# Expert rows gathered from x in plain float32, the first token half ahead, in a two-layer decoder trunk

## The chip, the core and the metric

One core of one Trainium2 chip. The metric is device time in microseconds of one execution, the median over runs. The program has five engines' instruction streams: PE (matmuls; PEld is its weight load), DVE (VectorE), ACT (ScalarE), POOL (GpSimd) and SP (sync), which issues the weight transfers in order.

## What is computed

Two layers over 256 tokens of width 1024, all in float32: a GLA and sparse-attention layer with a dense SwiGLU, then a Mamba-2 layer with a mixture of experts, then a closing norm. The change touches the last block alone:

```python
shift, scale, gate = adaln(c, moe_mod_w[i], moe_mod_b[i])
ffn = moe_ffn(modulate(x, moe_norm[i], shift, scale), moe_router[i], moe_w_gu[i], moe_w_down[i])
x = x + (gate * ffn).astype(x.dtype)
...
return rmsnorm(x, final_norm)
```

`modulate` is `rmsnorm(x, w) * (1 + scale) + shift`, one factor per token (the norm) and one scale and shift per channel. `moe_ffn` sends each token to the two experts with the largest router logits, each a SwiGLU of 1024 to 2 x 3584 to 1024, weighted by a softmax over the two.

## The kernel before

A tile layer schedules each engine's stream by priority and dependence; the order shown below is what it made, and each engine runs its stream in order.

**Tokens and slots.** The 256 tokens lie as two halves b = 0, 1 of 128 partitions in `x`. For each half the router's logits L are ranked on DVE (`rk`), `mk` marks the two chosen experts and a small PE product with a triangular matrix (L1205, L1207) gives `po_`, a token's slot number within its expert. Experts are worked in eight places; place 0 is always expert 0, the others are sorted by load. A place has three or two groups of 32 slots in turn (`NGS`), so 96 or 64 columns.

**Gather.** `gather(places)` makes `sl`, a 0/1 matrix tokens x slots, from `po_` and `mk` (L1229), and multiplies it with the normed tokens: for each of 8 channel blocks k, `xnh` and `xnl` (x times the norm factor, split into a high and a low float32r part by ACT L1359 and DVE L1360) for both halves, four matmuls (L1237, L1238). ACT and DVE apply scale and shift and write `gx` (L1242, L1244). Then it turns `sl` into slot rows `stT` (L1256) and gathers the mixing weights `gs` (L1265), which only the scatter at an expert's end needs. Place 0 is gathered ahead of everything; places 1 and 2 during place 0, 3 and 4 during place 2, and so on.

**Experts.** For each place and each of four chunks of the hidden width, `gate_up` multiplies `gx` with the weights in blocks of 1 MiB (L1276, output pa), four 32-row strips side by side; then silu and product (`sg`), a transpose (`turn_a`, `at`, L1310), and `down` (L1276, output pb). A three-group place has 12 matmuls per block, a two-group place 8. Plain float32 matmuls show as two records each. Each place has 42 blocks, 336 in all.

**Weights.** `load` (L238) takes the next buffer of a ring and issues a transfer on SP, which waits in order for the buffer's last reader. The ring has 6 + 3 buffers through the program, and 5 more (`raw3`) when the last stage's space becomes free; so 14 in the expert stage.

**Start of the stage.** `logits` transposes x by PE (L1176), copies it to SBUF (L1177) and multiplies with the router (L1180), for two column halves of each token half, during the last projection (L267 to L269); `dgs` holds each half's norm factor.

Of the kernel before, what the change touches and what calls it, by code (L numbers as in the profile page):

```python
# [8 lines left out]
F32 = mybir.dt.float32  # L9
# [12 lines left out]
NE = 8  # L22

CHUNKS = (1024, 1024, 1024, 512)
NS = 32
# [160 lines left out]
def trunk_kernel(ctx: ExitStack, tc: tile.TileContext, d: dict, out: bass.AP):  # L186
# [1000 lines left out]
    raws.append((ctx.enter_context(tc.tile_pool(name="raw3", bufs=5, side="right")), 5))  # L1187
    with ExitStack() as mx:
# [3 lines left out]
        L, rk, mk, po_ = (late.tile([128, 2, 8], F32, name=n) for n in ("L", "rk", "mk", "po_"))  # L1192
        c1, c2 = (late.tile([128, 8, 8], F32, name=n) for n in ("c1", "c2"))
        pp = pbank("pa")
        for b in range(2):
# [8 lines left out]
            mk_last = V.tensor_scalar(mk[:, b], rk[:, b], 1.5, None, op0=OP.is_lt)  # L1204
# [9 lines left out]
        iota = K("iota")  # L1214
# [3 lines left out]
        at_place = {}  # L1218

        def gather(places):  # L1220

            m_, p_, g_ = (mk, po_, ge) if places == (0,) else (mkp, pop, gep)
            sl = mw.tile([128, 2, 5 * NS], F32R, name="sl", bufs=1)
            off = [sum(NGS[q] for q in places[:i]) * NS for i in range(len(places) + 1)]
            W = off[-1]
            for b in range(2):
                for i, e in enumerate(places):
                    n = NGS[e] * NS
                    at_place["sl"] = V.tensor_scalar(sl[:, b, off[i]:off[i] + n], iota[:, :n], p_[:, b, e:e + 1],  # L1229
                                                     m_[:, b, e:e + 1], op0=OP.is_equal, op1=OP.mult)  # L1230
# [14 lines left out]
            yield  # L1245

# [3 lines left out]
            col = lambda b, g: sl[:, b, g * NS:(g + 1) * NS].bitcast(F32)  # L1250
# [134 lines left out]
        for _ in first:  # L1385
            pass
# [49 lines left out]
        for e in range(NE):  # L1436
            nxt = iter(())
            if e % 2 == 0:
                nxt = gather(tuple(range(e + 1, min(e + 3, NE))))
# [160 lines left out]
```

## Time and profile before

| | us |
|---|---|
| median of 3 runs | 1467.97 |
| lowest and highest | 1464.98, 1468.71 |
| profiled execution, its own time | 1465.52 |
| its span on the core | 1463.7 |
| PE busy in the span | 1412.7 |
| DMA moved | 493.66 MB, mean 337 GB/s |

A timeline row reads: start, length in us, engine, line, operation, output<-input, shapes, count of records, and in brackets the idle time of the engine before it and what ended it. PE rows include the drain of the last matmul, so neighbours overlap. A busy PE is not PE at its peak.

### The profile page before, as it was taken

The page shows a single profiled execution, that of the slowest core. Times are in us where ns is not written, and L with a number is a line of the kernel's source. Part 1 is how long each engine was busy: PE and PEld are TensorE (multiplying, and loading weights), DVE is VectorE, ACT ScalarE, POOL GpSimd, SP SyncE. Part 2 cuts the span into 40 slices and gives each one's busy share as a digit, 9 for nine tenths or more (in the row PEclk, how much of TensorE's full clock was granted, in tenths as well). Part 3 has the DMA queues.
Part 4 walks back from the last instruction along what each step waited for, and adds up shares of the span by engine and source line. Part 5 has one row for each costly group of instructions (what it writes and reads, how often), then busy time and mean ns, then how long its engine had stood idle before and what let it go on. Part 6 is the DMA issues. An engine that isn't in the chain of part 4 may idle for free.

```text
span 1463.7 us, 28534 instructions
## 1 busy us (share of the span) xinstructions
PE 1412.7 (97%) x12241; PEld 802.4 (55%) x12241; DVE 561.8 (38%) x1090; ACT 437.0 (30%) x856; POOL 5.3 (0%) x13
## 2 busy tenths in 40 slices
PE   7999999999999999999999999999999998999995
PEld 6876799999799987633433334333334323343321
DVE  7897688885678777510010110010100100100102
ACT  5577554444667785211000001000001000010001
POOL 0000000000000000000000000000000000000000
PEclk9999999999999999899999999999999999999998
DMA  9886778976544434699999999999999999999993
GB/s 383 345 303 259 300 295 334 363 289 228 207 173 148 141 116 172 235 358 357 370 421 419 419 419 420 418 420 419 420 419 418 420 419 419 419 420 418 419 420 148
DMA packets 68964, 493.66 MB, mean 337 GB/s; under 512 B 7648, under 2 KB 7904, under 8 KB 9568
## 3 DMA queue, kind: packets, MB, share of 16 engines
q1 hardware_dynamic: 68832, 491.77, 83.9%
q8 instruction: 98, 1.61, 0.4%
q14 instruction: 34, 0.28, 0.0%
HBM read 490.70 MB, written 1.05 MB: 336 GB/s over the span
## 4 chain that ended last, share of the span: by engine, by line
PE 80%; DMA 14%; ACT 3%; DVE 2%; issue 1%; SPq 0%; DVEq 0%; ACTq 0%
PE pa L1276 27%; PE pb L1276 12%; DMA raw<-in_e_gu_dram 7%; PE pa L267 7%; PE pa L268 7%; PE pa L269 7%; DMA raw<-in_e_gl_dram 4%; PE pb L268 3%; PE pb L269 3%; PE pb L267 3%; DMA raw<-in_e_dn_dram 3%; PE pc L1348 2%; PE pc L1310 1%; PE pb L400 1%; ACT wh L252 1%
## 5 line engine op out<-in xcount | busy, mean ns | idle before, releaser
L1276 PE MATMUL pa<-raw,gx 128*32 128x512 f32 (+1 forms) x5120 | 510.2, 540 | 7.3 <-DMA raw<-in_e_gl_dram 5.1
L1276 PEld LDWEIGHTS pa<-raw,gx 128*32 128x32 f32 x5120 | 167.1, 110 | 310.7 <-issue 258.4
L1276 PE MATMUL pb<-raw,at 128*32 128x512 f32 x2240 | 252.9, 594 | 4.3 <-DMA raw<-in_e_dn_dram 4.2
L1458 DVE TENSOR_TENSOR sg<-sg,pa 128x256 f32<-128x256 f32 (+1 forms) x80 | 31.0, 388 | 481.0 <-ACT sg L1457 479.3
L253 DVE TENSOR_TENSOR wl<-raw,wh 128x1024 fp32r<-128x1024 f32 (+1 forms) x155 | 185.3, 1204 | 57.1 <-ACT wh L252 56.9
L252 ACT CAST wh<-raw 128x1024 fp32r<-128x1024 f32 (+1 forms) x155 | 159.1, 1036 | 122.6 <-PE pb L268 53.0
L1276 PEld LDWEIGHTS pb<-raw,at 128*32 128x32 f32 x2240 | 70.8, 110 | 160.7 <-issue 141.1
L1457 ACT ACTIVATE sg<-pa 128x256 f32<-128x256 f32 (+1 forms) x80 | 28.6, 358 | 432.3 <-PE pa L1276 432.3
L267 PE MATMUL pa<-hh,wh 128*128 128x256 f32 (+1 forms) x392 | 112.4, 289 | 1.9 <-ACT wh L252 1.0
L268 PE MATMUL pa<-hl,wh 128*128 128x256 f32 (+1 forms) x392 | 111.4, 285 | 0.8 <-DVE hl L386 0.8
L269 PE MATMUL pa<-hh,wl 128*128 128x256 f32 (+1 forms) x392 | 111.3, 285 | 0.0
L267 PE MATMUL pb<-hh,wh 128*128 128x256 f32 (+1 forms) x360 | 101.7, 283 | 1.9 <-ACT hh L380 1.9
L268 PE MATMUL pb<-hl,wh 128*128 128x256 f32 (+1 forms) x360 | 102.5, 285 | 0.1
L269 PE MATMUL pb<-hh,wl 128*128 128x256 f32 (+1 forms) x360 | 101.8, 283 | 0.0
L281 DVE SCALAR_TENSOR_TENSOR junk<-raw,scb 128x1024 bf16<-128x1024 f32 x72 | 87.7, 1218 | 1.4 <-DMA raw<-in_hyb_mod_dram 0.8
L267 PEld LDWEIGHTS pa<-hh,wh 128*128 128x128 f32 (+1 forms) x392 | 73.7, 189 | 5.6 <-ACT wh L252 2.5
L268 PEld LDWEIGHTS pa<-hl,wh 128*128 128x128 f32 (+1 forms) x392 | 74.2, 189 | 2.1 <-DVE hl L386 0.9
L269 PEld LDWEIGHTS pa<-hh,wl 128*128 128x128 f32 (+1 forms) x392 | 74.0, 189 | 0.8 <-DVE gu L629 0.3
L1311 ACT COPY at<-pc 128x512 f32<-128x512 f32 (+2 forms) x32 | 17.5, 546 | 184.5 <-PE pc L1310 184.5
L267 PEld LDWEIGHTS pb<-hh,wh 128*128 128x128 f32 (+1 forms) x360 | 68.3, 190 | 2.9 <-ACT hh L380 2.1
L268 PEld LDWEIGHTS pb<-hl,wh 128*128 128x128 f32 (+1 forms) x360 | 68.3, 190 | 2.0 <-DVE hl L386 1.5
L269 PEld LDWEIGHTS pb<-hh,wl 128*128 128x128 f32 (+1 forms) x360 | 68.3, 190 | 0.1
(424 smaller groups left out, 1486.4 us busy)
## 6 DMA issues: line engine op xcount, KB each, us to landing
raw<-in_e_gu_dram SPq DMA_DIRECT2D x192, 1024.0 KB, 19.7
raw<-in_e_dn_dram SPq DMA_DIRECT2D x112, 1024.0 KB, 19.8
raw<-in_e_gl_dram SPq DMA_DIRECT2D x32, 1024.0 KB, 19.9
raw<-in_d_gu_dram SPq DMA_DIRECT2D x22, 1024.0 KB, 7.2
raw<-in_s_in_dram SPq DMA_DIRECT2D x20, 1024.0 KB, 4.8
raw<-in_hyb_mod_dram SPq DMA_DIRECT2D x12, 1024.0 KB, 9.9
raw<-in_ssm_mod_dram SPq DMA_DIRECT2D x12, 1024.0 KB, 6.4
raw<-in_d_dn_dram SPq DMA_DIRECT2D x11, 1024.0 KB, 7.9
```

The lines of the kernel that those rows point to most:

```text
L252: hi_last[0] = S.copy(hi[:, :n], r)
L253: lo_last[0] = V.tensor_sub(lo[:, :n], r, hi[:, :n].bitcast(F32))
L267: PE.matmul(ps, a[0], b[0], start=start, stop=False, **kw)
L268: PE.matmul(ps, a[0], b[1], start=False, stop=False, **kw)
L269: return PE.matmul(ps, a[1], b[0], start=False, stop=stop, **kw)
L281: V.scalar_tensor_tensor(jk, r[:, q * D:(q + 1) * D], 1.0, scb, op0=OP.mult, op1=OP.mult, accum_out=macc[m][:, 2 * j + q:2 * j + q + 1])
L400: PE.matmul(ps[:, o_ + b * 128:o_ + (b + 1) * 128], x[:, b, k * 128:(k + 1) * 128], dg[b], start=True, stop=True)
L1276: up_last[0] = PE.matmul(ps[32 * j:32 * j + 32, :rhs.shape[1]], lhs, rhs, start=start, stop=stop)
L1311: (V.tensor_copy if i else S.copy)(at[:, i:i + n].rearrange("p a n -> p (a n)"), pt_[:, :n * 128])
L1348: PE.matmul(pso[b], at_place[e, q][:, h, b], p[:, q], start=i == 0, stop=i == 2 * n - 1)
L1457: last = act(sg[:, r, :w], pg[r][:, :w], AF.Silu)
L1458: V.tensor_mul(sg[:, r, :w], sg[:, r, :w], pg[r][:, w:2 * w])
```

## The change

- The ring's last pool gets 7 buffers, 16 in all. Space for it comes from `xnh` and `xnl`, which go, and from `sg` and `at`, which are single now.
- Place 0 no longer goes through `gather`. For each half, as soon as its slots are known, DVE makes `s0`, the slot matrix times the token's norm factor (L1216), and PE multiplies x itself with it in plain float32 (L1218, 8 matmuls a half into two banks that stay open over both halves). ACT and DVE write `gx` from the two banks (L1232, L1234).
- Place 0's slot rows and mixing weights (`back`) come after its first chunk (L1446 is the gate's product ahead of them, L1283 the slot rows, L1292 the weights).
- A copy of x, `xc`, is made on ACT (L1476), since experts add to x while later places are gathered. Later gathers use `xc` and `sr`, the slot matrix times the norm factor, in plain float32: two matmuls per channel block (L1261) in place of four. Places 1 and 2 are gathered from the second chunk on.
- A fallback branch for overfull experts follows suit; it is not taken here.

```diff
-    raws.append((ctx.enter_context(tc.tile_pool(name="raw3", bufs=5, side="right")), 5))
+    raws.append((ctx.enter_context(tc.tile_pool(name="raw3", bufs=7, side="right")), 7))
...
+        pg0 = [pbank("pb") for _ in range(2)]
+        s0 = mp.tile([128, 2, CAP], F32, name="s0")
+        rx = mp.tile([128, 2], F32, name="rx")
         pp = pbank("pa")
         for b in range(2):
...
+
+            V.tensor_scalar(mr[:, b], rk[:, b], 1.5, dgs[b][0], op0=OP.is_lt, op1=OP.mult)
             V.tensor_copy(po_[:, b], pp[:, 8 * b:8 * b + 8])
+            V.tensor_scalar(s0[:, b], iota[:, :CAP], po_[:, b, 0:1], mr[:, b, 0:1], op0=OP.is_equal, op1=OP.mult)
+            for k in range(KD):
+                PE.matmul(pg0[k // 5][:, k % 5 * CAP:(k % 5 + 1) * CAP], x[:, b, k * 128:(k + 1) * 128], s0[:, b],
+                          start=b == 0 and k % 5 == 0, stop=b == 1, skip_group_check=True)
...
+        for k in range(KD):
+            src = pg0[k // 5][:, k % 5 * CAP:(k % 5 + 1) * CAP]
+            if k % 2:
+                act(gx[:, 0, k], src, AF.Identity, bias=B[:, k:k + 1], scale=A[:, k:k + 1])
+            else:
+                V.tensor_scalar(gx[:, 0, k], src, A[:, k:k + 1], B[:, k:k + 1], op0=OP.mult, op1=OP.add)
+
+        xc = mp.tile([128, 2, D], F32, name="xc")
...
+            sl, off = slots(places)
+            W = off[-1]
+            sr = mw.tile([128, 2, 5 * NS], F32, name="sr", bufs=1)
+            for b in range(2):
+                V.tensor_scalar(sr[:, b, :W], sl[:, b, :W], rx[:, b:b + 1], None, op0=OP.mult)
             for k in range(KD):
                 if k % 2 == 0:
                     yield
-                pgx = pbank("pb" if places == (0,) and k % 4 > 1 else "pc")
-                ks = slice(k * 128, (k + 1) * 128)
+                pgx = pbank("pc")
                 for b in range(2):
-                    PE.matmul(pgx[:, :W], xnh[:, b, ks], sl[:, b, :W], start=b == 0, stop=False)
-                    PE.matmul(pgx[:, :W], xnl[:, b, ks], sl[:, b, :W], start=False, stop=b == 1)
+                    PE.matmul(pgx[:, :W], xc[:, b, k * 128:(k + 1) * 128], sr[:, b, :W], start=b == 0, stop=b == 1)
...
             yield
+            back(places, sl, off)
+
+        def back(places, sl, off):
...
-            at = mw.tile([128, 2 * NG, 128], F32, name="at")
+            at = mw.tile([128, 2 * NG, 128], F32, name="at", bufs=1)
...
-        first = gather((0,))
-        next(first)
-        xnh = mp.tile([128, 2, D], F32R, name="xnh")
-        xnl = mp.tile([128, 2, D], F32R, name="xnl")
-        for b in range(2):
-            for hf in range(2):
-                s = slice(hf * 512, hf * 512 + 512)
-                with tc.issue_after(ex_last[0].ins), tc.issue_after((at_place["sl"] if b or hf else mk_last).ins):
-                    act(xnh[:, b, s], x[:, b, s], AF.Copy, scale=dgs[b][0])
-                    V.scalar_tensor_tensor(xnl[:, b, s], x[:, b, s], dgs[b][0], xnh[:, b, s].bitcast(F32),
-                                           op0=OP.mult, op1=OP.subtract)
...
-                    if i == 2:
+                    if i == 2 and (e, c) != (0, 0):
                         next(nxt, None)
-                sg = mw.tile([128, NG, 256], F32, name="sg")
+                sg = mw.tile([128, NG, 256], F32, name="sg", bufs=1)
...
                 if (e, c) == (0, 0):
                     with tc.issue_after(up_last[0].ins):
                         moe_gate()
-                next(nxt, None)
+                        for b in range(2):
+                            S.copy(xc[:, b], x[:, b])
+                        back((0,), *slots((0,)))
+                else:
+                    next(nxt, None)
```

How the streams change, in the words of the two programs. PE at the router's last steps; `pb<-cs,x` is a transpose of x, `pc<-ra,hh` the router's product. Before:

```order
L1176 MATMUL pb<-cs,x 128x128 x4
L1205 MATMUL pa<-mk,cs 128x8
L1207 MATMUL pa<-mk,cs 128x8
L1365 MATMUL pa<-mk,cs 128x8
L1180 MATMUL pc<-ra,hh 128x8 x4
L1176 MATMUL pb<-cs,x 128x128 x4
L1180 MATMUL pc<-ra,hh 128x8 x4
L1237 MATMUL pc<-sl,xnh 128x96 x2
```

The same place after:

```order
L1176 MATMUL pb<-cs,x 128x128 x4
L1210 MATMUL pa<-mk,cs 128x8
L1212 MATMUL pa<-mk,cs 128x8
L1380 MATMUL pa<-mk,cs 128x8
L1176 MATMUL pb<-cs,x 128x128
L1180 MATMUL pc<-ra,hh 128x8 x4
L1176 MATMUL pb<-cs,x 128x128 x3
L1218 MATMUL pb<-s_6353,x 128x96 x5
L1180 MATMUL pc<-ra,hh 128x8 x4
```

One transpose of the last column half moved ahead of a router product, and five of the first token half's eight gather matmuls stand ahead of the other. PE from the end of the first gather to the end of expert 0's first chunk, before (`pa<-raw,gx` are the expert's blocks):

```order
L1238 MATMUL pb<-sl,xnl 128x96
L1256 MATMUL pc<-cs,sl 32x128 x16
L1276 MATMUL pa<-raw,gx 32x512
L1265 MATMUL pc<-ge,sl 32x1 x16
L1276 MATMUL pa<-raw,gx 32x512 x95
L1431 MATMUL pc<-cs,mac_moe 32x128 x16
L1237 MATMUL pc<-sl,xnh 128x160
```

And after:

```order
L1218 MATMUL pb<-s_6353,x 128x96 x3
L1210 MATMUL pa<-mk,cs 128x8
L1380 MATMUL pa<-mk,cs 128x8
L1218 MATMUL pb<-s_6353,x 128x96 x8
L1303 MATMUL pa<-raw,gx 32x512 x96
L1446 MATMUL pc<-cs,mac_moe 32x128 x16
L1283 MATMUL pc<-cs,sl 32x128 x8
L1303 MATMUL pa<-raw,gx 32x512
L1283 MATMUL pc<-cs,sl 32x128 x8
L1292 MATMUL pc<-ge,sl 32x1 x16
```

The slot rows moved behind the first 96 block matmuls, the gate's product with them. SP at the first loads into the new pool, with what each waits for, before:

```order
L238 DMA raw<-in_e_gu_dram 128x2048 [waits DMAHW3_49,PE_49,Pool_49]
L238 DMA raw<-in_e_gu_dram 128x2048 [waits DMAHW4_49]
L238 DMA raw<-in_e_gu_dram 128x2048 [waits DMAHW5_49]
L238 DMA raw<-in_e_gu_dram 128x2048 [waits DMAHW6_49]
L238 DMA raw<-in_e_gu_dram 128x2048 [waits DMAHW7_49]
L238 DMA raw<-in_e_gu_dram 128x2048 [waits DMAHW0_49,PE_49]
L238 DMA raw<-in_e_gu_dram 128x2048 [waits DMAHW1_49,PE_49]
L238 DMA raw<-in_e_dn_dram 128x2048 [waits DMAHW2_49,PE_49]
```

And after:

```order
L238 DMA raw<-in_e_gu_dram 128x2048 [waits DMAHW3_49,PE_49,Pool_49]
L238 DMA raw<-in_e_gu_dram 128x2048 [waits DMAHW4_49]
L238 DMA raw<-in_e_gu_dram 128x2048 [waits DMAHW5_49]
L238 DMA raw<-in_e_gu_dram 128x2048 [waits DMAHW6_49]
L238 DMA raw<-in_e_gu_dram 128x2048 [waits DMAHW7_49]
L238 DMA raw<-in_e_gu_dram 128x2048 [waits DMAHW0_49]
L238 DMA raw<-in_e_gu_dram 128x2048 [waits DMAHW1_49]
L238 DMA raw<-in_e_dn_dram 128x2048 [waits DMAHW2_49,PE_49]
```

The sixth and seventh load into the pool lost their wait for PE; the eighth keeps one, on a buffer of an earlier pool.

## Rows read from the trace of the kernel before

**Rows 1.** Table of stretches: us, busy per engine, granted clock, DMA share, GB/s

```profile
605.00:610.00 5.00, 5.00 (x74) 3.21 (x77) 2.95 (x17) 3.39 (x6) 0.00 (x0) 0.52 0.10 39
610.00:615.00 5.00, 5.00 (x52) 1.80 (x48) 2.83 (x16) 0.00 (x0) 0.00 (x0) 1.00 0.30 87
...
610.00:730.00 120.00, 119.91 (x1287) 45.80 (x1283) 12.76 (x46) 12.51 (x31) 0.00 (x0) 1.00 0.92 352
730.00:1443.00 713.00, 695.81 (x6771) 243.23 (x6763) 73.42 (x160) 60.74 (x142) 0.00 (x0) 1.00 1.01 416
```

**Rows 2.** The chain that ended last, its end: start, us, what

```profile
1423.51 20.45 DMA raw<-in_e_dn_dram
...
1444.00 1.97 PE pb L1276 x16
```

**Rows 3.** Waits of the sync queue, 580 to 615: us in total, times, longest

```profile
SPq L238 <- PE pa L269: 11.2, 1, 11.2
...
SPq L238 <- PE pa L1276: 20.4, 2, 18.3
```

**Rows 4.** Timeline of the sync queue, expert 0 and the turn to expert 1

```profile
612.40 2.90 SPq L238 DMA_DIRECT2D raw<-in_e_gu_dram  x2
617.55 8.05 SPq L238 DMA_DIRECT2D raw<-in_e_dn_dram  x4
...
733.62 5.48 SPq L238 DMA_DIRECT2D raw<-in_e_dn_dram  x4
```

**Rows 5.** Line L238, the loads, from 520 to 640: issue to landing

```profile
DMA to landing us min/median/max: 4.7/5.0/13.3
```

**Rows 6.** Timeline of PE in expert 0: a gather step, four blocks, slot rows

```profile
643.93 0.34 PE L1237 MATMUL pc<-sl,xnh 128*128 128x160 f32 x1
...
644.78 0.28 PE L1238 MATMUL pc<-sl,xnl 128*128 128x160 f32 x1
644.98 10.51 PE L1276 MATMUL pa<-raw,gx 128*32 128x512 f32 x96
...
689.53 1.06 PE L1256 MATMUL pc<-cs,sl 128*32 128x128 f32 x32
...
691.84 0.58 PE L1265 MATMUL pc<-gep,sl 128*32 128x1 f32 x48
```

**Rows 7.** Timeline of PE at the router's last steps and the first block

```profile
592.54 1.06 PE L1180 MATMUL pc<-ra,hh 128*128 128x8 f32 x8
...
594.87 1.06 PE L1180 MATMUL pc<-ra,hh 128*128 128x8 f32 x8 [0.78 <-DVE hh L1177]
...
607.29 1.06 PE L1276 MATMUL pa<-raw,gx 128*32 128x512 f32 x1
```

**Rows 8.** Timeline of DVE, the second half's rank chain

```profile
592.33 0.68 DVE L454 TENSOR_TENSOR x<-x,res 128x512 f32<-128x512 f32 x1
594.12 0.69 DVE L1177 COPY hh<-pb 128x512 f32<-128x512 f32 x1 [1.11 <-PE pb L1176]
...
595.97 0.23 DVE L1196 TENSOR_REDUCE L<-pc 128x8 f32<-128x64 f32 x1 [1.08 <-PE pc L1180]
...
598.02 0.17 DVE L1204 TENSOR_SCALAR mk<-rk 128x8 f32<-128x8 f32 x1
...
599.12 0.32 DVE L1229 TENSOR_SCALAR sl<-cs,po__6347,mk 128x96 fp32r<-128x96 f32 x1
```

**Rows 9.** Timeline of PE, plain float32 matmuls L400 at two places

```profile
8.49 6.43 PE L400 MATMUL pb<-dg,x 128*128 128x128 f32 x32 [8.49 <-DVE dg L390]
...
182.33 1.16 PE L400 MATMUL pb<-dg,x 128*128 128x128 f32 x8
```

**Rows 10.** Table of stretches around the fall and rise of the clock

```profile
596.00:597.00 1.00, 0.43 (x2) 0.46 (x3) 0.93 (x5) 0.73 (x2) 0.00 (x0) 0.59 1.07 451
...
609.00:610.00 1.00, 1.00 (x31) 0.60 (x33) 0.33 (x4) 0.73 (x1) 0.00 (x0) 0.58 0.00 0
```

**Rows 11.** Costliest groups: ACT's cast of 128x1024

```profile
L252 ACT CAST wh<-raw 128x1024 fp32r<-128x1024 f32 (+1 forms) x155 | 159.1, 1036 | 122.6 <-PE pb L268 53.0
```

More of the change, by code (lines that the diff above doesn't have):

```diff
@@ L1190, in trunk_kernel @@
         mw = mx.enter_context(tc.tile_pool(name="moew", bufs=2))
-        L, rk, mk, po_ = (late.tile([128, 2, 8], F32, name=n) for n in ("L", "rk", "mk", "po_"))
+        L, rk, mk, mr, po_ = (late.tile([128, 2, 8], F32, name=n) for n in ("L", "rk", "mk", "mr", "po_"))
         c1, c2 = (late.tile([128, 8, 8], F32, name=n) for n in ("c1", "c2"))
+        iota = K("iota")
+        pg0 = [pbank("pb") for _ in range(2)]
+        s0 = mp.tile([128, 2, CAP], F32, name="s0")
+        rx = mp.tile([128, 2], F32, name="rx")
         pp = pbank("pa")
@@ L1218, in trunk_kernel, with slots, gather @@
         at_place = {}
[L1220 to L1223 removed]
+        for k in range(KD):
[5 more added lines that the diff above has]
+        xc = mp.tile([128, 2, D], F32, name="xc")
+        def slots(places):
+            m_, p_ = (mk, po_) if places == (0,) else (mkp, pop)
+            sl = mw.tile([128, 2, 5 * NS], F32, name="sl", bufs=1)
             off = [sum(NGS[q] for q in places[:i]) * NS for i in range(len(places) + 1)]
[L1225 removed]
             for b in range(2):
                 for i, e in enumerate(places):
[L1228 to L1230 removed]
+                    V.tensor_scalar(sl[:, b, off[i]:off[i + 1]], iota[:, :off[i + 1] - off[i]], p_[:, b, e:e + 1],
+                                    m_[:, b, e:e + 1], op0=OP.is_equal, op1=OP.mult)
+            return sl, off
+        def gather(places):
+            sl, off = slots(places)
[3 more added lines that the diff above has]
+                V.tensor_scalar(sr[:, b, :W], sl[:, b, :W], rx[:, b:b + 1], None, op0=OP.mult)
             for k in range(KD):
@@ L1383, in trunk_kernel @@
             V.scalar_tensor_tensor(ge[:, b], f0[:, b], v0[:, 0, b:b + 1], tm[:, b], op0=OP.mult, op1=OP.add)
-        for _ in first:
-            pass
+        for b in range(2):
+            V.tensor_copy(rx[:, b:b + 1], dgs[b][0])
         nt = mp.tile([128, 8], F32, name="nt")
@@ L1436, in trunk_kernel @@
         for e in range(NE):
-            nxt = iter(())
-            if e % 2 == 0:
-                nxt = gather(tuple(range(e + 1, min(e + 3, NE))))
+            nxt = gather(tuple(range(e + 1, min(e + 3, NE)))) if e % 2 == 0 else iter(())
             if e:
@@ L1461, in trunk_kernel @@
                         moe_gate()
-                next(nxt, None)
+                        for b in range(2):
+                            S.copy(xc[:, b], x[:, b])
+                        back((0,), *slots((0,)))
+                else:
+                    next(nxt, None)
                 if prev:
@@ L1489, in final @@
             y = [x_rstd(0)]
[L1490 removed]
+            jk = mw.tile([128, 512], F32, name="sg", bufs=1)
             V.scalar_tensor_tensor(jk, x[:, 1, h1], 1.0 / D, x[:, 1, h1], op0=OP.mult, op1=OP.mult,
@@ L1527, in trunk_kernel @@
                         for b in range(2):
-                            PE.matmul(pgx[:, :128], xnh[:, b, ks].bitcast(F32), s2[:, b], start=b == 0, stop=False)
-                            PE.matmul(pgx[:, :128], xnl[:, b, ks].bitcast(F32), s2[:, b], start=False, stop=b == 1)
+                            PE.matmul(pgx[:, :128], xc[:, b, ks], s2r[:, b], start=b == 0, stop=b == 1)
                         V.tensor_scalar(g2[:, k], pgx[:, :128], A[:, k:k + 1], B[:, k:k + 1], op0=OP.mult, op1=OP.add)
```

17 lines of the change are left out of this document (9 added, 8 removed).

## The prediction

> **What bounds the kernel now.** I read the table of stretches first. From 730 to 1443 us the DMA share is 1.01 and 416 GB/s are moved; from 610 to 730 it is 0.92 and 352, and in 605 to 615 the share is 0.10 and 0.30 [rows 1]. The chain of waits ends in the same sense: its last long pieces are transfers of 20 us, and after the last one only 16 matmul records and the closing norm remain [rows 2]. So from 730 us on, the end is a fixed distance behind the weight stream: 336 transfers of 1 MiB, 2.52 us each at 416 GB/s. Nothing that PE, ACT or DVE save there counts. What counts is how much transfer time is lost before the stream runs without holes. That loss lies in 596 to 735 us. The DMA queue's own waits show it: the sync queue stood 11.2 us until the last projection matmul L269, which frees the space of the new buffers, issued five loads, and then stood 20.4 us in two waits for the first expert's matmuls L1276 [rows 3]: all 14 buffers were full and none free.
>
> Behind that hole PE is the pace. The timeline of the sync queue has issues at 612.40 and, two to a 2.90 us row of which the last 0.33 is the issue itself, every 2.57 us; four dn loads take 8.05 us, the same 2.57 [rows 4]. That is one 1 MiB block of a three-group expert on PE: 96 records of L1276 (four blocks of 12 matmuls, two records each) take 10.51 us with the drain of the last [rows 6]. It is slower than the 2.52 us of a transfer, and gathers and transposes come on top, so in all of expert 0 each load is issued when PE frees a buffer, and lands 4.7 to 5.0 us later [rows 5]. At 733.62 the spacing has become 1.72 us [rows 4], the two-group expert 1, and the transfers are again the slower ones. A load n is therefore issued when block n minus the number of buffers is done, and the end of the kernel moves with that.
>
> **Part by part.**
>
> *Two more weight buffers (14 to 16).* Load n waits for block n-16, no longer for block n-14, and those are two blocks of 2.57 us apart on PE: 5.1 us earlier for every load of the PE-paced stretch. The order of the sync queue shows that both are usable at once: the two extra loads carry no wait for PE, and the load ahead of the seven waits for the same instruction as before. They fill the 10 us hole, in which 5.0 us of transfer fit. The space paid for them costs nothing on the path: sg and at, now single, are each written only when PE's own order has their last reader behind it. **+5.1 us.** Bounds: 0 (a rival below) and 5.1.
>
> *First expert's rows earlier.* Before, b=1's router logits (second L1180 at 594.87) lead over DVE's rank chain (595.97, 598.02) to the slot matrix at 599.12 [rows 7, 8]; then 32 matmuls over the two halves hi and lo, then the transposed slot rows L1256 and L1265, and the first L1276 at 607.29 [rows 7]. In the new order one transpose stands ahead of the first L1180 of b=1 and has to wait for x, ready at 593.01 (592.33 + 0.68), where L1180 began at 592.54; this shifts the hh copy of 594.12 by some 0.5 us [rows 7, 8]. Five of the new first-half matmuls then stand ahead of the second L1180. A plain float32 matmul of this form costs 0.25 us at full clock: L400, 8 records for 4 matmuls in 1.16 us, less the last record's drain; at the program's start 32 records (16 matmuls) took 6.43 us, 0.40 each [rows 9]. So the second L1180 goes from 594.87 to about 595.9, and b=1's slot matrix, which has one more small DVE operation ahead of it in the chain and the mr one, from 599.12 to about 600.4, done at 600.7. Eight matmuls remain: 2.0 us at full clock, 3.3 at low, and expert 0 starts at 602.7 or 604.1. DVE's first gx piece stands behind some ten small operations of 0.15 to 0.2 us and is ready at about 602.5, so it is not later than PE; the other seven are needed one per block.
>
> The clock decides what that start is worth. The granted clock fell at 596.2 (0.59 over 596 to 597), after PE had gaps between the router's steps, and was back at 609.8 (0.58 over 609 to 610) [rows 10]: 13.7 us at 1.2 instead of 2.4 GHz, through narrow matmuls, and up again 2.5 us after the first expert matmul. The second free buffer came at 614.97; two blocks of 2.57 back is 609.8, the start that before is worth at full clock. For the changed kernel I take the same rise, 2.5 us after the start at 604.1: half of 2.5 us is lost, so it is worth a start at 605.4. **+4.4 us.** Bounds: 7.1 (no fall: 602.7) and 1.1 (the clock falls in the new gap at about 599.6 and stays low for the same 13.7 us, to 613.3: 604.1 + 4.6 = 608.7).
>
> *First slot rows deferred.* They do not vanish: 16 L1256 and 16 L1265 now stand in PE's stream after expert 0's first chunk, where PE is the pace. The later set of 24 and 24 gives the price: 32 records of L1256 in 1.06 us, and two thirds of 0.58 [rows 6]. **-1.5 us**; up to -2.5 if PE also stands for the two pc banks that ACT empties between them. The two xc copies (ACT, 128x1024) stand between the router's copies, where ACT waits for PE and DVE, and cost nothing; were that cover gone, one pass of 1.04 us (a cast of that size [rows 11]) would go onto the start.
>
> *Gathers of experts 1 and 2.* Each of four steps runs 8 single-pass matmuls from 643.93 to 644.98, 1.05 us [rows 6]. Now 4 plain float32 ones; scaled by columns from L400, 0.25 x 160/128 = 0.31 us each, 1.25 us. Four steps lose 0.2 to 0.25 each: **-1.0 us.** Bounds: 0 (same time as now) and -3.8 (0.40 us as at low clock, 0.50 scaled, 2.0 a step). The Trainium skill, page "FP8 and Floating Point Precision", section "TensorE Precision Notes", says that true FP32 takes 4 passes through the array, which speaks against this change: two such matmuls would be eight passes where four single ones stood. By that rule alone a step doubles and the four lose 4.2 us, sum 3.8; the trace does not bear it out at this width, since L400's plain float32 matmul, of 128 columns, takes 0.25 us against 0.13 for one of the four single ones. The later gathers (experts 3 to 7) lie under the transfers: free.
>
> *Removed work on ACT and DVE* (xnh, xnl: four passes each): it was on the path to the first gather and is inside the start term; elsewhere it is hidden.
>
> **Sum:** 5.1 + 4.4 - 1.5 - 1.0 = 7.0 us. Against the profiled execution: span 1463.7 to 1456.7, time 1465.5 to 1458.5. That execution lies 2.5 us under the median of the three runs; from the median 1468.0 the forecast is **1461.0 us**. The next thing late is then still PE's pace in expert 0, up to about 730 us.
>
> **Rivals.**
> 1. *The clock does not fall, or returns within the gather:* the new first-half matmuls close PE's gap at 594 to 596, where it fell. For: dense float32 work stands there. Against: a new idle of about 2.5 us before b=1's matmuls. Start 7.1: gain 9.7, **1458.3**.
> 2. *The low clock only moves:* it falls in that new idle and lies on the expert's own blocks for as long as before. Start 1.1: gain 3.7, **1464.3**.
> 3. *PE sets the end, not the transfers:* PE reads 119.91 of 120 us and 695.81 of 713 us busy [rows 1]; then buffers bring nothing and only 4.4 - 2.5 is left, **1466.1**. Against it: a DMA share of 1.01 and the transfers in the chain.
> 4. *Plain float32 at twice the time:* PE holds the buffers of expert 0 for 3.2 us more, gain 3.8, **1464.2**. Against: the L400 row.
> 5. *Slower:* the low clock holds on through expert 0's first chunk. A block at half clock costs 5.15 instead of 2.57 us and each microsecond of it loses half. With 2.5 us against for the moved work and 5.1 for the buffers, the gain is gone if it lasts 16.6 us from 604.1, to 620.7; over the whole chunk of eight blocks it loses 20.6 and gives about **1480**. For: nothing but the fall itself; against: before, it rose 2.5 us after these same matmuls began.
>
> That the buffers or the early half are not really early is shut out by the order of the two programs.
>
> **How the numbers follow.** Forecast 0.50, rival 1 0.15, rival 2 0.17, rival 3 0.08, rival 4 0.05, rival 5 0.05. The forecast's own range is 1458.5 to 1463.5. For 8 in 10 the range takes in rivals 1 and 2 and the scatter of the runs before (1465.0 to 1468.7), and most of rival 3: 1456 to 1466. 0.3% is 4.4 us, about what a measurement of this kernel tells from no change: under 1463.6 is faster. Faster: the forecast, rival 1, and the better edge of 2: 0.70. Same: most of 2, 3 and 4: 0.25. Slower: 0.05.
>
> **What the profile will show.** The sync queue's wait for L1276 in 600 to 615 falls from 20.4 to under 10 us, with seven loads, not five, issued behind L269. First expert matmul at 602.5 to 604.5, after 16 new float32 matmuls. The clock row says which rival holds: low till about 606.6 for the forecast. The gather steps of expert 0 at 1.2 to 1.3 us, the moved slot rows after the eighth block. DMA share 1.01 reached some 7 us earlier in the program and unchanged after. Wrong would be: holes in the stream after 740 us, a first expert matmul later than 606, or an end that does not follow the last transfer by the same 20 us.

## The result, and the profile after

| | before | after |
|---|---|---|
| median of 18 runs each, side by side | 1468.84 | 1461.37 |
| lowest and highest | 1463.66, 1472.81 | 1456.38, 1467.96 |
| ratio, 95% interval | | 0.995 (0.9936 to 0.9964) |
| profiled execution: its time, its span | 1465.52, 1463.7 | 1462.21, 1460.3 |
| the same once more (e11, e12): time, span | 1465.01, 1463.0 | 1454.99, 1453.1 |

The forecast was 1461.0 with a range of 1456 to 1466. The whole interval of the ratio lies below 0.997, so by the bound of 0.3% the change is faster. In a later session the changed kernel had 1459.1 against 1469.84, ratio 0.9932 (0.9909 to 0.9954).

The stretches of the changed kernel (columns as in [rows 1]):

```profile
605.00:610.00 5.00, 4.50 (x24) 4.24 (x28) 2.77 (x20) 0.20 (x1) 0.00 (x0) 0.50 1.00 424
610.00:615.00 5.00, 5.00 (x36) 1.30 (x40) 4.13 (x21) 2.79 (x5) 0.00 (x0) 0.74 0.92 387
610.00:730.00 120.00, 120.00 (x1314) 44.77 (x1314) 17.52 (x68) 16.33 (x39) 0.00 (x0) 0.99 0.93 358
730.00:1443.00 713.00, 702.46 (x6821) 248.25 (x6818) 74.17 (x164) 61.44 (x143) 0.00 (x0) 1.00 1.00 415
```

Against [rows 1], the hole is gone: in 605 to 615 the DMA share is 1.00 and 0.92 where it was 0.10 and 0.30. The new buffers came free 4.3 us later in this execution than in that of before (more on this below), so the 30 us from there on, before and after, tell it better:

```profile
591.50:621.50 30.00, 27.76 (x244) 17.80 (x246) 15.94 (x74) 9.16 (x19) 0.00 (x0) 0.77 0.71 278
```

```profile
595.80:625.80 30.00, 27.95 (x202) 15.87 (x204) 13.22 (x69) 6.57 (x13) 0.00 (x0) 0.77 0.97 385
```

The share rose from 0.71 to 0.97. The long stretch is as before, 415 GB/s. The sync queue's waits in 590 to 618, to be read beside [rows 3], and its timeline, beside [rows 4]:

```profile
SPq L238 <- PE pa L1303: 16.9, 2, 14.8
SPq L238 <- PE pa L269: 11.2, 1, 11.2
```

```profile
595.80 3.41 SPq L238 DMA_DIRECT2D raw<-in_e_gu_dram  x7
614.07 8.05 SPq L238 DMA_DIRECT2D raw<-in_e_dn_dram  x4
624.37 22.21 SPq L238 DMA_DIRECT2D raw<-in_e_gu_dram  x8
```

Seven loads go out at 595.80, not five, and the first load that needs a freed buffer goes out at 614.07. The expert's matmuls, L1276 before, are L1303 now.

One thing must be known before spans are compared. Executions of one and the same program differ by several us ahead of all that the change touches: the release of the new buffers, the first issue behind L269, came at 591.50 and 591.61 in the two of before, at 595.80 and 591.54 in the two of after. In the first of after the clock is at half in four short stretches far upstream, three of them here:

```profile
87.00:91.00 4.00, 4.00 (x35) 1.56 (x35) 4.00 (x9) 2.53 (x7) 0.00 (x0) 0.58 1.09 403
380.00:384.00 4.00, 3.44 (x15) 3.37 (x16) 3.40 (x7) 1.43 (x3) 0.00 (x0) 0.57 1.00 420
404.00:408.00 4.00, 4.00 (x23) 4.00 (x22) 4.00 (x7) 2.89 (x8) 0.00 (x0) 0.57 0.01 4
```

So all that follows is counted from the release. From it to the end of the span, before takes 872.2 and 871.4 us, after 864.5 and 861.6: 7.7 us less in the first pair, 9.8 in the second, and the spans of the second pair, with releases 0.07 us apart, show the 9.9 directly.

### The profile page after: what moved, and what is told of

Read it like the earlier page. It is cut to its first block, busy times and chain, and to the rows that moved or that the text cites. A ratio compares the mean times of both kernels' runs of the same rounds, so it can differ in the third digit from the quotient of the medians.

```text
span 1460.3 us, 28550 instructions
## 1 busy us (share of the span) xinstructions
PE 1416.4 (97%) x12241; PEld 807.4 (55%) x12241; DVE 562.3 (39%) x1100; ACT 436.2 (30%) x854; POOL 5.3 (0%) x13
## 3 DMA queue, kind: packets, MB, share of 16 engines
HBM read 490.70 MB, written 1.05 MB: 337 GB/s over the span
## 4 chain that ended last, share of the span: by engine, by line
PE 93%; DVE 2%; DMA 2%; ACT 2%; issue 0%; SPq 0%; ACTq 0%; DVEq 0%
PE pa L1303 33%; PE pb L1303 16%; PE pa L267 7%; PE pa L268 7%; PE pa L269 7%; PE pb L268 3%; PE pb L269 3%; PE pb L267 3%; PE pc L1375 2%; PE pc L1337 1%; PE pc L1261 1%; DMA raw<-in_e_dn_dram 1%; PE pb L702 1%; DMA raw<-in_hyb_mod_dram 1%; ACT wh L252 1%; PE pa L732 1%
## 5 line engine op out<-in xcount | busy, mean ns | idle before, releaser
L1303 PE MATMUL pa<-raw,gx 128*32 128x512 f32 (+1 forms) x5120 | 507.7, 541 | 0.0
L1303 PEld LDWEIGHTS pa<-raw,gx 128*32 128x32 f32 x5120 | 166.9, 110 | 301.1 <-issue 262.0
L1303 PE MATMUL pb<-raw,at 128*32 128x512 f32 x2240 | 253.0, 594 | 2.2 <-DMA raw<-in_e_dn_dram 2.2
L1303 PEld LDWEIGHTS pb<-raw,at 128*32 128x32 f32 x2240 | 70.5, 110 | 154.1 <-issue 144.2
L269 PE MATMUL pa<-hh,wl 128*128 128x256 f32 (+1 forms) x392 | 112.6, 289 | 0.0
L269 PE MATMUL pb<-hh,wl 128*128 128x256 f32 (+1 forms) x360 | 102.2, 284 | 0.0
L269 PEld LDWEIGHTS pa<-hh,wl 128*128 128x128 f32 (+1 forms) x392 | 75.3, 192 | 0.8 <-DVE gu L629 0.3
L269 PEld LDWEIGHTS pb<-hh,wl 128*128 128x128 f32 (+1 forms) x360 | 68.7, 191 | 0.3
## 6 DMA issues: line engine op xcount, KB each, us to landing
raw<-in_e_gl_dram SPq DMA_DIRECT2D x32, 1024.0 KB, 18.3
```

The costliest lines, as they stand in the source:

```text
L269: return PE.matmul(ps, a[1], b[0], start=False, stop=stop, **kw)
L1303: up_last[0] = PE.matmul(ps[32 * j:32 * j + 32, :rhs.shape[1]], lhs, rhs, start=start, stop=stop)
```

## The experiments

All are variants of the changed kernel, but for e11. Times in us from the release; "low" is the stretch at 1.2 GHz around the router, start and length, by the clock record of the trace; "first freed" is the issue of the first load that waits for an expert's block; "PE to end" runs from the first expert matmul to the end of the span.

| | low | first expert matmul | first freed | PE to end | median | ratio to before |
|---|---|---|---|---|---|---|
| before | 4.7, 13.7 | 15.8 | 20.9 | 856.4 | 1468.84 | |
| before again, e11 | 5.0, 13.7 | 15.8 | 21.1 | 855.6 | | |
| after | 3.1, 13.7 | 14.1 | 18.3 | 850.4 | 1461.37 | 0.995 (0.9936 to 0.9964) |
| after again, e12 | 8.5, 6.8 | 12.1 | 16.5 | 849.5 | 1459.1 | 0.9932 (0.9909 to 0.9954) |
| e1, 14 buffers | 8.4, 6.8 | 12.1 | 16.5 | 855.0 | 1466.92 | 0.9999 (0.9984 to 1.0013) |
| e2, slot rows early | 8.2, 6.8 | 12.9 | 17.9 | 848.8 | 1460.86 | 0.9951 (0.993 to 0.9971) |
| e3, copies late | 6.4, 6.8 | 12.0 | 15.4 | 848.7 | 1457.85 | 0.9933 (0.9913 to 0.9952) |
| e4, first half late | 3.4, 13.7 | 13.7 | 18.2 | 850.6 | 1461.14 | 0.9953 (0.9933 to 0.9973) |
| e5, other order | 4.8, 10.2 | 11.8 | 16.3 | 850.2 | 1460.27 | 0.9932 (0.9909 to 0.9955) |
| e6, fillers | 4.9, 10.2 | 12.4 | 16.5 | 850.5 | 1457.53 | 0.9921 (0.9897 to 0.9945) |
| e7, gathers twice | 3.2, 13.7 | 14.1 | 18.3 | 862.9 | 1476.9 | 1.0041 (1.0023 to 1.0059) |
| e9, 17 buffers | 4.9, 10.2 | 12.3 | 16.5 | 848.2 | 1458.99 | 0.9923 (0.9902 to 0.9945) |
| e10, 17 and order | 4.8, 10.2 | 11.8 | 16.3 | 848.3 | 1456.28 | 0.9907 (0.9888 to 0.9926) |

e8 has another release and stands with its own experiment. The medians come from four sessions, in which the kernel before had 1468.84 (after), 1467.83 (e1 to e4), 1469.02 (e5 to e8) and 1469.84 (e9, e10, e12), so between sessions the ratios are to be compared. "PE to end" still holds what is left of the low clock: that stretch ends 1.3 us after the first expert matmul in e3, 2.0 in e8, 2.1 in e2 and 2.5 to 3.3 in the others.

**e1: the two buffers taken back.**

```diff
-    raws.append((ctx.enter_context(tc.tile_pool(name="raw3", bufs=7, side="right")), 7))
+    raws.append((ctx.enter_context(tc.tile_pool(name="raw3", bufs=5, side="right")), 5))
```

> The changed kernel with 14 weight buffers instead of 16 (five in the third pool, as before the change); all else stays. Theory (the weight stream sets the end, and in expert 0 PE paces it by freeing buffers): every load is issued two blocks of 2.57 us later, so 5.1 us longer than the changed kernel, about 1466.5 (ratio to the kernel before 0.998 to 0.999); the sync queue issues five loads, not seven, behind the last projection matmul and stands some 5 us longer for the first expert's matmuls. Rival (PE's own work sets the end, buffers bring nothing): no longer than the changed kernel, 1461.4, ratio 0.995.

Measured: 1466.92, 5.5 us over the changed kernel's 1461.37 (by the ratios, 0.9999 against 0.995, 7.2). PE to end is 855.0 against 849.5 of e12, whose start is the same to 0.1 us: 5.5 us. The theory holds, and rival 3 of the prediction falls for this change. By the ratio to before, 0.9999, the rest of the change alone is worth nothing that can be told. Its profiled execution says otherwise: with the low clock of 6.8 us it ends 867.0 us after the release, 4.3 to 5.2 less than the two of before. How often the low clock is that short is not known, so this stays open.

**e2: the slot rows ahead of the first chunk again.**

```diff
                         for b in range(2):
                             S.copy(xc[:, b], x[:, b])
-                        back((0,), *slots((0,)))
...
             V.tensor_copy(rx[:, b:b + 1], dgs[b][0])
+        back((0,), *slots((0,)))
```

> The deferral alone undone: the first expert's transposed slot rows stand again ahead of its first chunk (eight of them while PE waits for the second token half, eight behind the gather, the gate column after five expert matmuls), in place of behind the chunk. Theory: the 2.6 us by which PE's stretch in expert 0 got longer shrink by the moved rows' 1.5 to 2.5 us, and the start loses about the same, since eight rows and the gate column now stand at low clock ahead of the eighth block: 1461 to 1463, first expert matmul 0.5 to 1.5 us later, counted from the release of the buffers. Rival A (the deferral is what makes the start early): 2 us longer or more, 1463.5 to 1465. Rival B (deferral is a pure loss, the rows fit PE's waits): 1459 to 1460.

Measured: 1460.86, no difference that can be told. The trace has both halves of it. The stretch that holds the moved rows in the changed kernel (the row of 22.21 us above) shrinks by 2.0:

```profile
622.21 20.20 SPq L238 DMA_DIRECT2D raw<-in_e_gu_dram  x8
```

and the first freed load comes 1.4 us later than in e12 with a low clock of the same length (17.9 against 16.5). By these rows rivals A and B fall both (the median alone does not shut out B, 1459 to 1460): the deferral moves a cost of 1.4 to 2 us from one end of the first chunk to the other.

**e3: the two x copies later; e4: the first token half later as well.**

```diff
-                        for b in range(2):
-                            S.copy(xc[:, b], x[:, b])
+                        with tc.issue_after(ex_last[0].ins):
+                            for b in range(2):
+                                S.copy(xc[:, b], x[:, b])
```

> The changed kernel with the two copies of x for the later gathers (ACT, 1.05 us each) held behind ACT's last exponential of the router's norm. In the trace of the changed kernel the first one (595.77) stands ahead of the copy of the transposed x of the second token half's first part (596.73, its transposes ended at about 596.15). Theory: this copy cost the router's chain about 0.6 us, so the second router product and the first expert matmul come 0.5 to 0.8 us earlier, counted from the release of the buffers, 1460.7. Rival: the chain is held by the last part of x (597.32) alone, nothing moves: first expert matmul within 0.2 us of the changed kernel's 14.1 us after the release.

This one is here because of two rows of ACT in the changed kernel:

```profile
595.77 1.05 ACT L1476 COPY xc<-x 128x1024 f32<-128x1024 f32 x1 [1.96 <-PE pa L269]
596.73 0.58 ACT L1177 COPY hh<-pb 128x512 f32<-128x512 f32 x1
```

The hh copy's transposes (4 records of L1176 from 595.57, 0.60 us) were done at 596.17, and the copy began at 596.73, behind the xc copy. With the copies late, the rank matmul of the second half came 6.8 us after the release instead of 7.3 in e1 (all of PE's matmuls ahead of it at full clock in both), and the first freed load 1.0 us earlier than in e1 and e12. The first expert matmul moved by only 0.1, since the low clock began 2 us sooner and was over sooner. So of the first freed load's gain a part is the clock's.

The edit also changed PE's order, as the rows of the changed kernel and of e3 show:

```profile
597.47 0.30 PE L1176 MATMUL pb<-cs,x 128*128 128x128 f32 x1 [0.73 <-DVE x L454]
597.61 0.96 PE L1180 MATMUL pc<-ra,hh 128*128 128x8 f32 x8
```

```profile
599.69 1.06 PE L1180 MATMUL pc<-ra,hh 128*128 128x8 f32 x8
600.60 0.64 PE L1176 MATMUL pb<-cs,x 128*128 128x128 f32 x4
```

In the changed kernel one transpose stands ahead of the product and waits for x (ready at 597.32); the hh copy ended at 597.31, so without the xc copy the product could not have come earlier in that order. In e3 the product is ahead of all four transposes and starts 1.05 us after the release, not 1.81. The 0.5 us belong to the late copies and this order together; neither was tried alone. Median 1457.85 against 1461.37 and 1459.1: the sign is as expected, the size within the scatter.

```diff
-            for k in range(KD):
-                PE.matmul(pg0[k // 5]...
+            with tc.issue_after(lg_last[0].ins):
+                for k in range(KD):
+                    PE.matmul(pg0[k // 5]...
```

> As e3, and the eight float32 matmuls of the first token half held behind the last router product, so that they fill PE's wait in the second half's rank chain and no longer stand ahead of the product. Theory: the start is lost on the router's chain, 1.05 us by the five first-half matmuls ahead of the product (it could start when its copy ended at 599.67, and began at 600.72) beside the 0.6 us of e3: first expert matmul 12.3 to 12.8 us after the release instead of 14.1, every load 1.5 us earlier, 1459.8. Rival (the clock decides): PE has less to do between 596 and 600, the clock falls sooner or stays low as long after the first expert matmul, and the second router product and the gather at low clock eat the gain: first expert matmul 13.5 to 14.1 us after the release, 1461 to 1462.

Measured: first expert matmul 13.7 us after the release, 1461.14: the times are the rival's. Its reason is not shown: in this execution the clock was low for 13.7 us from 3.4 on, but so it was, from 3.1 on, in the first of after, where the first-half matmuls stand early. Beside that one the gain is 0.1 to 0.4 us.

**e5: another order in the router; e6: fillers against the fall of the clock.** Both have the late copies of e3. e5 holds the product of the last part but one back behind the last transposes, and all first-half matmuls behind the last product. e6 adds three matmuls that nothing reads:

```diff
+                with tc.issue_after(tr_last[0].ins):
+                    PE.matmul(fb[0][:, :384], ident, x[:, 0, :384], start=True, stop=True)
...
+                with tc.issue_after(g_last.ins):
+                    PE.matmul(fb[0][:, :256], ident, x[:, 0, :256], start=True, stop=True)
...
+                with tc.issue_after(tris_last.ins):
+                    PE.matmul(fb[0][:, :192], ident, x[:, 0, :192], start=True, stop=True)
```

> No fillers: the order alone. x copies late as in e3; PE transposes the last part of x before, not behind, the router product of the part ahead of it; all first-half matmuls stand behind the last product. Theory (the start is PE's order in the router's chain): first expert matmul 11.0 to 11.6 us after the release of the buffers where the clock is low for 6.8 us, 13.0 to 13.5 where it is low for 13.7 (12.1 and 14.1 for the changed kernel's order in two executions). End 1458 to 1459.5. Rival (only the length of the low clock counts, and that is the chance of an execution): no different from the changed kernel in the median, 1460 to 1462.

> As e5, with three float32 matmuls into an unused bank (384, 256 and 192 columns) in PE's waits between the last projection matmul and the second half's gather; their result is read by nothing. Theory (the clock falls because PE has little to do in the router's chain): the clock no longer falls, or only once for 6.8 us and later; the second half's 8 float32 matmuls take 2.0 instead of 3.7 us and the first freed buffer's load is issued 12.5 to 14 us after the release, instead of 18.3 (low for 13.7 us) and 16.4 (6.8 us) in the changed kernel's order: 1456.5 to 1458.5. Rival (the narrow router matmuls count as nothing, and the fall comes as before): low stretch as in e5, plus up to 0.5 us for the fillers, 1459 to 1461.

Measured: the clock fell 4.8 us after the release in e5 and 4.9 in e6, for 10.2 us in both, and the first freed load went out at 16.3 and 16.5. The fillers did nothing but take their time (0.55 us at the first expert matmul), and the theory of e6 falls in this form: these three fillers are not what keeps the clock up. With e5's order the first expert matmul comes at 11.8, the earliest of all up to here; with a low clock of 10.2 us its first freed load goes out at 16.3, where the changed kernel's order needs the shorter 6.8 us for 16.5. The medians (1460.27, 1457.53) can't be told apart: e5's lies in its rival's range, and that e6's lies in its theory's is chance, since the clock did not do what the theory says.

**e7: each gather matmul twice.**

```diff
-                for b in range(2):
+                for b in (0, 1, 0, 1):
                     PE.matmul(pgx[:, :W], xc[:, b, k * 128:(k + 1) * 128], sr[:, b, :W], start=b == 0, stop=b == 1)
```

> Each float32 gather matmul of the later experts runs twice (the second pass writes the same sums again); all else is the changed kernel. It prices the plain float32 gather and shows which steps lie on the path. Theory: 4 matmuls more a step at 0.31 to 0.33 us, so the four steps in expert 0 take 2.5 to 2.6 instead of 1.29 us and every load behind them comes 5.0 to 5.3 us later, while the twelve steps of the later experts are free: 1466.5 (ratio 0.998 to 0.999). Rival A (later gathers count too): 16 steps, up to 20 us, 1475 or more. Rival B (PE's expert 0 is no pace any more with 16 buffers): 1461.4 to 1463.

Measured: 1476.9, 15.5 us over the changed kernel (by the ratios 13.4; from the first expert matmul to the end, 862.9 against 850.4, 12.5). The theory falls, and the time is that of rival A, by which the later gathers count too. One gather step, in the changed kernel and in e7 (PE):

```profile
656.42 1.35 PE L1261 MATMUL pc<-sr,xc 128*128 128x160 f32 x8
657.71 2.78 PE L1303 MATMUL pb<-raw,at 128*32 128x512 f32 x24
```

```profile
659.17 2.44 PE L1261 MATMUL pc<-sr,xc 128*128 128x160 f32 x16
```

Four more matmuls take 1.09 us, 0.27 each. The four steps of expert 0 cost 4.2 us on PE's stretch (116.2 instead of 112.0), and the landing of the last load comes 4.4 us later from the release: that part is as expected. But the twelve later steps are not free, though rival A's price for them was too high. Four of them have 64 columns and not 160 (changed kernel, then e7):

```profile
1274.83 1.10 PE L1261 MATMUL pc<-sr,xc 128*128 128x64 f32 x8
```

```profile
1289.07 2.00 PE L1261 MATMUL pc<-sr,xc 128*128 128x64 f32 x16
```

From the last landing (1448.39) to the end, e7 takes 27.1 us where the changed kernel takes 19.0. Eight times 1.09 and four times 0.90 are 12.3 us that the later steps add, and 8.1 show up behind the stream: PE had only about 4 us in hand behind the transfers. The next three runs use that up from the other side.

**e8, e9, e10: a 17th buffer.**

```diff
-    raws.append((ctx.enter_context(tc.tile_pool(name="raw3", bufs=7, side="right")), 7))
+    raws.append((ctx.enter_context(tc.tile_pool(name="raw3", bufs=8, side="right")), 8))
...
-        gx = mp.tile([128, 4, KD, CAP], F32, name="gx")
+        gx = mp.tile([128, 3, KD, CAP], F32, name="gx")
...
-            stT = mw.tile([128, len(quads), 2, 2, 128], F32R, name="stT", padded_shape=[128, 3, 2, 2, 128])
+            stT = [mw.tile([128, 2, 2, 128], F32R, name="stT", bufs=5) for _ in quads]
```

> The changed kernel with a 17th weight buffer (eight in the third pool; the place comes from three instead of four slots of gathered rows, five single transposed-row tiles, and slot tiles in buffers that nothing else uses by then). Theory: one more block of 2.57 us, as each of the two before: 1458.8, eight loads issued behind the last projection matmul, and the queue still stands some 10 to 13 us for the first expert's matmuls. Rival (the hole behind the release is full, since each load takes 2.5 us of transfer and the eight fill 20 us, more than the 18.3 or 16.4 us to the first freed buffer): the eighth gains less than 2.57, 1459.5 to 1461.4.

Measured: 1458.71, ratio 0.9927 (0.9902 to 0.9952). The eight loads went out 5 us late, since the pool now reaches into the tile of the transposed x, and all of it is released by the router's last product:

```profile
SPq L238 <- PE pc L1180: 16.2, 1, 16.2
```

It cost nothing: PE to end was 848.2. The median is the theory's, but the 17th buffer did not bring the theory's whole block (below); that it brings less is the rival's, for another reason than the rival's full hole. The last blocks of PE say why. Before, PE waited for a load ahead of each of the last eleven blocks (eight of the last ten in e11); in the changed kernel ahead of the last four (three in e12); in e8 ahead of none (timeline of PE, before, after, e8):

```profile
1418.44 1.92 PE L1276 MATMUL pb<-raw,at 128*32 128x512 f32 x16 [0.62 <-DMA raw<-in_e_dn_dram]
1421.03 1.93 PE L1276 MATMUL pa<-raw,gx 128*32 128x256 f32 x32 [0.67 <-DMA raw<-in_e_gl_dram]
1423.43 1.93 PE L1276 MATMUL pa<-raw,gx 128*32 128x256 f32 x32 [0.47 <-DMA raw<-in_e_gl_dram]
```

```profile
1429.69 3.64 PE L1303 MATMUL pb<-raw,at 128*32 128x512 f32 x32
1433.87 1.92 PE L1303 MATMUL pb<-raw,at 128*32 128x512 f32 x16 [0.54 <-DMA raw<-in_e_dn_dram]
1436.34 1.92 PE L1303 MATMUL pb<-raw,at 128*32 128x512 f32 x16 [0.55 <-DMA raw<-in_e_dn_dram]
```

```profile
1425.20 7.08 PE L1303 MATMUL pb<-raw,at 128*32 128x512 f32 x64
1432.83 3.64 PE L1303 MATMUL pb<-raw,at 128*32 128x512 f32 x32 [0.55 <-ACT at L1338]
```

With 17 buffers PE's own work sets the end. e9 and e10 put this to the test: the 17th buffer as a pool of its own, with the late copies of e3 and with the order of e5. Five loads go out 5 us earlier than in e8, and the next three 3 us earlier (4.5 to 5.4 us after the release; they still wait for the router). In e8 and e9 all first-half matmuls stand behind the last product, as in e4.

```diff
-    raws.append((ctx.enter_context(tc.tile_pool(name="raw3", bufs=8, side="right")), 8))
+    raws.append((ctx.enter_context(tc.tile_pool(name="raw3", bufs=7, side="right")), 7))
+    raws.append((ctx.enter_context(tc.tile_pool(name="raw4", bufs=1, side="right")), 1))
```

> The 17 buffers of e8, the 17th as a pool of its own, so that the first seven are released by the last projection matmul and only the last by the last router product; and the late copies of x of e3. Theory (in e8 PE never waits for a load in the last expert, so PE's own work now sets the end): the earlier release of seven buffers brings nothing, only PE's earlier start does, 0.5 to 1 us against e8: 1457.5 to 1458.5, and PE again waits for no load in the last expert. Rival (the stream still sets the end): the seven transfers that start 5 us earlier bring up to 5 us, 1453 to 1455.

> e9 with the router order of e5 (last transposes ahead of the product, all first-half matmuls behind the last product). Theory (PE's start is what is left): 1456 to 1458, at or a little under e9. Rival (stream): as e9, 1453 to 1455, no difference between the two.

Measured: PE to end 848.2 and 848.3, as in e8, where the loads went out 3 to 5 us later. The stream's rival falls; the end is now the first expert matmul plus 848.2. Against e12's 849.5 the 17th buffer is worth 1.3 us; e10 against e5, with the same order and the same low clock, gives 1.9, and e9 against e3, whose low clock ended sooner after the first expert matmul, 0.5. That is less than a block of 2.57, and by these rows an 18th is worth nothing (it wasn't run). e10 has the lowest median of all, 1456.28, ratio 0.9907 (0.9888 to 0.9926); in its profiled execution it ends at 1451.8, against 1453.1 for e12 with a release 0.14 us apart. It beats the kernel before; against the changed kernel of the same session (e12) the intervals overlap.

**e11, e12: both kernels once more, with no edit.**

> The kernel before, a second profiled execution: how long is the low clock behind the last projection matmul, and when is the first freed buffer's load issued? Theory (the low clock is set by when it falls, which differs between executions): low for 13.7 us again, or for 6.8 to 10.3 us, and with the shorter stretch the first freed buffer's load 1.5 to 2 us earlier than 20.9 us after the release. Rival (the kernel before has the long stretch by its order): low 13.7 us, load within 0.3 us of 20.9.

> The changed kernel again, beside the others on one chip. Theory: 1460 to 1462, ratio 0.994 to 0.996; the first freed buffer's load 18.3 us after the release if the clock is low for 13.7 us, 16.4 if for 6.8, between them for 10.2. Rival (the start is fixed by the instructions): 18.3 us whatever the clock does.

Measured: before had the long low stretch again (the rival of e11, and its theory allows it too), after had the short one and its first freed load at 16.5 (the theory of e12; its median, 1459.1, came out 0.9 us under the range expected). The clock in the two of after, the first one and e12 (stretches; the clock is the third number from the end):

```profile
599.00:612.00 13.00, 11.67 (x56) 9.68 (x58) 7.30 (x44) 2.52 (x9) 0.00 (x0) 0.50 1.01 426
```

```profile
591.00:599.00 8.00, 5.76 (x51) 5.40 (x49) 5.03 (x23) 3.60 (x7) 0.00 (x0) 1.00 0.82 307
600.00:606.00 6.00, 6.00 (x28) 4.02 (x32) 3.82 (x25) 2.36 (x6) 0.00 (x0) 0.50 1.01 427
607.00:615.00 8.00, 8.00 (x80) 2.22 (x76) 2.98 (x15) 0.00 (x0) 0.00 (x0) 1.00 1.01 419
```

and PE's rows in the same two, at the same instructions:

```profile
598.78 2.14 PE L1218 MATMUL pb<-s,x 128*128 128x96 f32 x10
600.72 1.77 PE L1180 MATMUL pc<-ra,hh 128*128 128x8 f32 x8
...
606.26 3.73 PE L1218 MATMUL pb<-s,x 128*128 128x96 f32 x16 [0.49 <-DVE s L1216]
609.92 4.51 PE L1303 MATMUL pa<-raw,gx 128*32 128x512 f32 x28
```

```profile
594.51 1.25 PE L1218 MATMUL pb<-s,x 128*128 128x96 f32 x10
595.61 0.98 PE L1180 MATMUL pc<-ra,hh 128*128 128x8 f32 x8
...
599.96 3.71 PE L1218 MATMUL pb<-s,x 128*128 128x96 f32 x16 [0.50 <-DVE s L1216]
```

At low clock the five first-half matmuls and the product take 2.14 and 1.77 us, at full clock 1.25 and 0.98; the second half ran at low clock in both. The low clock is worth 1.8 us of start between two executions of one program (18.3 and 16.5).

## Why the prediction was right, and where its terms were off

| term | forecast | after against before | e12 against e11 |
|---|---|---|---|
| start: first freed load, 20.9 - 18.3 and 21.1 - 16.5 | 4.4 | 2.6 | 4.6 |
| two buffers: two blocks, 617.55 - 612.40 [rows 4] | 5.1 | 5.15 | 5.15 |
| moved rows and gathers on PE's stretch | -2.5 | -2.6 | -2.6 |
| sum | 7.0 | 5.2 | 7.1 |
| release to end, measured | | 7.7 | 9.8 |

- **What bounds the kernel** was read rightly: the hole after the release, PE's pace in expert 0, then the stream. e1 shows the buffers at 5.5 us for 5.1, and seven loads go out behind L269 as said. The wait for the first expert fell from 18.3 us [rows 3] to 14.8, and not, both waits together, "from 20.4 to under 10 us": with the start 4.4 us earlier the first freed load goes out at 608.0, and with seven issues that end at some 594.5 that is 13.5 us of wait by the prediction's own numbers. This sign in the profile was worked out wrongly, the term was not.
- **The start** is the term that was mis-sized, in the profiled execution of after: 2.6 for 4.4, within its bounds of 1.1 to 7.1. The step that failed there is the clock ahead of the router's last product. The forecast had that product and the five matmuls ahead of it at full clock: "So the second L1180 goes from 594.87 to about 595.9", 4.4 us after the release. The clock fell 3.1 us after the release, ahead of most of them; the product came at 4.9, and the first expert matmul at 14.1 for the 12.6 of the forecast. In e12, where the clock fell 8.5 us after, the product came at 4.1, the first expert matmul at 12.1, and the start is worth 4.6. The xc copies, which were to "cost nothing", did hold the hh copy by 0.56 us, but by the rows under e3 the transposes' wait for x, which the forecast had, covers this. The rise, 2.7 us after the first expert matmul (609.92 to 612.59), was as taken from before. Of the signs of being wrong, "a first expert matmul later than 606" did come (609.92); counted from before's release it is 605.6, so that sign was set on a time that the release alone can move.
- **Deferred rows and gathers** came out as forecast in sum, -2.6 on PE's stretch in expert 0 (112.0 for 109.4 from the second freed load to the 41st). By e2 the rows are 2.0 of it, for the forecast 1.5 within its bound of 2.5; each gather step went from 1.05 [rows 6] to 1.29 us (656.42 to 657.71), the forecast 0.2 to 0.25. Rows and steps taken singly make 3.0, and where the 0.4 between is does not show. By e7 a plain float32 matmul of 160 columns costs 0.27 us, where the estimate from L400 [rows 9] had 0.31. The rule of the Trainium skill, page "FP8 and Floating Point Precision", section "TensorE Precision Notes" (four passes for true FP32), would have doubled a step only if a float32r matmul were a single pass; the prediction took it so, and the page does not say it. The rows have 0.27 us against 0.13 for one of the float32r matmuls replaced, twice and not four times. That speaks against the rule and the assumption taken together; which of the two does not hold here no run shows.
- **The rest**, 2.5 to 2.7 us, was in no term. From the landing of the 56th expert load to the last landing, before took 708.0 and 706.4 us, after 706.6 and 705.7, the variants 704.8 to 707.7: by that, 0.7 to 1.4 us that may be scatter of the stream. The tail from the last landing to the end is 0.7 to 0.8 us shorter in after, and that lies behind its last transfer: up to the landing of the last output the tails are alike (16.2 and 16.1 us, 16.5 and 15.8), and from there to the end it is 3.5 and 3.3 before, 2.5 and 2.8 after, 2.5 to 3.3 in the variants. The cause of neither was tried, and what is left of the rest (0.4 and 1.2 us, in expert 0) has no row either: this stays open. In the first pair this made up for the start; that the median came out 0.4 us from the forecast is in part luck.
- **Rivals.** The clock did not stay up (1), and more work on PE of the kind tried in e6 does not hold it up. That the low clock only moves (2) holds for neither execution as written: in the first the clock fell sooner than before (3.1 us after the release, not 4.7), and the start lost on the router's chain; in e12 it fell in the new gap, at 8.5 where the rival has 599.6 (8.1), but stayed low for 6.8 us and not 13.7. PE as the bound (3) is false at 14 to 16 buffers by e1, but the sentence that nothing saved on PE counts behind 730 us held by a margin of some 4 us only: e7 goes beyond it and e8 uses it up. Plain float32 at twice the time (4) and the slow clock through the first chunk (5) did not occur.

## What to carry to other kernels

A prefetch buffer is worth one block of the stage that paces the releases, until the consumer no longer waits for a load at the end: count those waits in the last blocks (eleven, four, none) to see how many buffers more will pay. Work called free because it lies under a stream is free up to the slack of its engine, here about 4 us in 710, and that slack shrinks with each gain on the stream's side. When executions of one program differ by more than the effect, compare them from a common event, here the release of the buffers.

## What was not expected of the hardware

- The clock at the same instructions differs between executions of one program: it fell 3.1 or 8.5 us after the release and stayed low for 13.7 or 6.8 us, worth 1.8 us of start. It fell in the first of after with PE never idle for more than 0.73 us since the last projection matmul, among matmuls of 8 columns, transposes and the first of 96 columns.
- Half-clock stretches of 3.4 or 6.8 us upstream, present in one execution and absent in another, go with releases from 594.0 to 598.6 us; where there are none, it comes at 591.5 to 591.8. Of the 7.2 us between the spans of the two executions of after, 4.3 lie ahead of the release; a part of the scatter of the times is likely to come from there.
